# From the MLP's up products to its down products: a PSUM tile of its own for the last product, other memory for the first loads, and the last relu one step later

## The chip, the core and the metric

The kernel runs on one core of one Trainium2 chip. The metric is device time in microseconds (us), the median of the runs. Besides, one execution was recorded by the hardware profiler; its times are those of the views below. PE is TensorE's matrix multiply, PEld its weight load, DVE is VectorE, ACT is ScalarE, SP the queue that issues loads. Line numbers (L170) are those of the kernel before.

## What is computed

The reference is a two-layer trunk on a sequence of 1024 rows of width 1024, in float32. Layer 0 mixes with a gated short convolution, layer 1 with latent attention; each has an MLP with a squared relu and a hidden width of 4096.

```python
def short_conv_mixer(h, w_in, w_conv, b_conv, w_out):
    bcx = h @ w_in
    b_gate, c_gate, xh = jnp.split(bcx, 3, axis=-1)
    u = c_gate * xh
    conv = depthwise(u, w_conv) + b_conv
    return (b_gate * conv) @ w_out

def squared_relu_mlp(h, w_up, w_down):
    return jnp.square(jax.nn.relu(h @ w_up)) @ w_down

for l in range(DEPTH):
    mod = c_act @ ada_w[l] + ada_b[l]
    ...
    x = x + g_m[:, None, :] * rmsnorm(y, norm_g[l, 1])
    h = modulate(rmsnorm(x, norm_g[l, 2]), sh_f, sc_f)
    y = squared_relu_mlp(h, mlp_up_w[l], mlp_down_w[l])
    x = x + g_f[:, None, :] * rmsnorm(y, norm_g[l, 3])
```

The change lies where `h @ w_up` ends and `@ w_down` begins, once in each layer, and where `h @ w_in` of the conv mixer ends.

## The kernel before

**Precision.** Every float32 operand is split into a high part (an ACT copy, L173) and a low part (a DVE subtraction, L174). `mm` (L170) makes three matmuls of one product: low x high, high x low, high x high. The two operations of a split can only be used in that order, and a matmul waits for the part it reads.

**The up products.** `mlp_up` works on pairs of 128-column blocks of `w_up`, 16 pairs a layer. For each pair, `all_pairs` forms a 2 x 2 block product with seven products instead of eight (Winograd's scheme). A product (`prod`) is 4 x 3 = 12 matmuls with 512 columns. The operands of the activations are named "11", "21", "22", "t1" to "t4"; those of the weights are `w`, `t2`, `s2` and `t3`. After the two products of `w`, the order on PE within a pair is: product 6 (s2 with operand t2) into bank `x_`; product 7 (t3 with operand t3) into a second bank, `v`; product 5 (t2 with t1), added into `x_`; and, put off into the next pair, product 3 (`second`, t3 with 22), added into `x_`, and product 4 (`fourth`, t2 with t4), added into `v`. Between them partial sums are taken out: `take(u2)` and `take(u4)` (L581) copy `x_` on ACT after products 6 and 5, `u4 += v` follows on DVE (L594), `third` evicts `x_` after product 3 (L1217, a relu), and `last` adds `v` to `u2` (L609). Product 3 cannot start before `take(u4)` has read `x_`. PSUM has four such banks ("one"), two for each pair, used in turn.

For the last pair there is no next pair: `mlp_up` calls `second` and `fourth` at once and leaves the rest (`last`, `third`) to the down stage. `last` ends with `done`, which is `store`: two relus and two squares on ACT (L1221 to L1225), and a `late` entry whose DVE sums (L1236 to L1239) and seven stores to the DRAM arrays `ha[0]` to `ha[6]` (L1241, issued from ACT's queue) are made when `flush` is called. The conv mixer's input products run through the same `all_pairs`; there the steps of the last job are called in reverse order of the list.

**The down products.** `down_pairs` makes seven products too, in the order 0, 1, 3, 6, 4, 5, 2, each over seven steps i. A step loads a block of `w_down` into its own place (only in products 0, 1, 3, 6) and 512 KB of `ha` into one of four raw tiles, splits both into *rings* (the weight side alternates between two rings, the other side goes round three), and makes 24 matmuls into four banks. The order of SP's loads is fixed to that of the program (`pinned`). Over the first three steps a list `before` is worked off from its end, with ACT's and DVE's order fixed as written (`pinned`): each step's two splits first, then one entry. Entry of step 0: `third`, then `last` with `store`; of step 1: nothing; of step 2: `flush`. So ACT works through step 0's high parts, `third`, the relus and squares, step 1's high parts, and so on.

**The memory of the blocks.** `room` gives each block of 4 KB (per partition) its place in a pool: `sl` on the left, `sd` on the right. `sd` is laid over memory that the up stage used: from its front over the up stage's weight pool `up` (split weights, then two raw tiles that only every third pair uses, then s2), and behind that over the operands of the activations in the order "11", "21", t2, t3. A load into such a place waits for the last reader of the old contents.

**Background tasks.** `bg` is a list of tasks for the next stage's modulation vectors. For each vector eight of ten tasks load 512 KB of `ada_w` (or `kv_ada_w`) into a raw tile and add it, scaled, on DVE (L195); the last makes 16 small matmuls (L214). `down_pairs` of layer 0 has four vectors, 40 tasks; `run_bg(1 + (i % 3 == 0))` takes one or two a step in every product but the first. In layer 1 the list is empty there.

Of the kernel before, what the change touches and what calls it, by code (L numbers as in the profile page):

```python
# [17 lines left out]
P = 128  # L18
# [43 lines left out]
def trunk_kernel(ctx: ExitStack, tc: tile.TileContext, x, c, ada_w, ada_b, norm_g, conv_in_w, conv_w,  # L62
# [5 lines left out]
    def nm(s):  # L68
        uid[0] += 1
        return f"{s}_{uid[0]}"  # L70
# [176 lines left out]
    def run_bg(n):  # L247
        for _ in range(min(n, len(bg))):
            bg.pop(0)()
# [289 lines left out]
    def prod(out_, which, ops, first=True, kks=range(4)):  # L539
        w, k0, name = which  # L540
        for kk in kks:
            mm(out_, (w[0][:, k0 + kk, :], w[1][:, k0 + kk, :]), ops[name][kk], first and kk == 0, kk == 3, not first)
# [4 lines left out]
    def all_pairs(up, ops, jobs):  # L547

        end = []
        for raws, begun, quarter, done, between in jobs:
            ready = raws()
            a = begun if begun is not None else row_tile()
            p1 = a[:, HALF:] if begun is not None else None
            x_ = bank_ps()
            if begun is None:
                w = up_split(up, ready[0])  # L560
                prod(x_, (w, 0, "11"), ops)
                nc.scalar.activation(a[:, :HALF], x_, AF.Copy)
                if end:
                    end.pop()()
                y_ = mm_ps()
                prod(y_, (w, 4, "21"), ops)
                if end:
                    end.pop()()
                nc.vector.tensor_tensor(a[:, :HALF], a[:, :HALF], y_, op=ALU.add)
            rest = {}  # L570
            if isinstance(ready, dict):
                rest = ready
            else:
                for part in pair_sums(up, *ready):
                    rest.update(part or {})
            b = row_tile()
            u2, u4 = halves(b)

            def take(dst):
                if p1 is None:  # L580
                    nc.scalar.activation(dst, x_, AF.Copy)  # L581
                else:
                    nc.vector.tensor_tensor(dst, p1, x_, op=ALU.add)

            prod(x_, rest[6], ops, begun is not None)
            take(u2)
            while end:
                end.pop()()
            between()
            v = bank_ps()  # L590
            prod(v, rest[7], ops)
            prod(x_, rest[5], ops, False)
            take(u4)
            nc.vector.tensor_tensor(u4, u4, v, op=ALU.add)  # L594

            def second(x_=x_, rest=rest):
                prod(x_, rest[3], ops, False)

            def third(x_=x_, p1=p1, a=a, quarter=quarter):
                if p1 is None:  # L600
                    quarter(a, x_)
                else:
                    nc.vector.tensor_tensor(p1, p1, x_, op=ALU.add)

            def fourth(v=v, rest=rest):
                prod(v, rest[4], ops, False)

            def last(v=v, u2=u2, a=a, b=b, done=done):
                nc.vector.tensor_tensor(u2, u2, v, op=ALU.add)  # L609
                done(a, b)  # L610

            end += [last, third, fourth, second]
        return end

    def up_mm(w, h, kk=KD, steps=None):
# [169 lines left out]
    def down_pairs(ys, wd, before):  # L785

        sd = pool("sd", "right")  # L790
        n = PAIRS // 2
        w4 = wd[ROWS * P:, :].rearrange("(q two p) d -> p q two d", two=2, p=P)
        sl = pool("sl")
        ws = [{} for _ in range(n)]

        def room(q, b, i0, i1):
            for i in range(i0, i1):
                ws[i][b] = q.tile([P, 2, HALF], F32, name=nm("w"))

        room(sl, "12", 0, n)  # L800
        room(sl, "11", n - 5, n)
        room(sd, "22", 0, n)
        room(sd, "21", 1, n)
        rings = [sd.tile([P, 2, 2, HALF], F32R, name=nm("ring")) for _ in range(5)]
        room(sd, "11", 0, n - 5)
        room(sd, "21", 0, 1)
        pbs = [rings[2], rings[0]]
        spares = [rings[1], rings[3], rings[4]]
        pas = [spares[(7 * n - 1 - j) % 3] for j in range(3)]
        count = 0  # L810

        def get(i, b):
            ld(ws[i][b], w4[:, 2 * i:2 * i + 2, int(b[0]) - 1, (int(b[1]) - 1) * HALF:int(b[1]) * HALF])

        def less(i, b, x_, y_):
            nc.vector.tensor_tensor(ws[i][b], ws[i][x_], ws[i][y_], op=ALU.subtract)

        def spot(half, t, col):
            return ys[4 * half + t][:, col * HALF:(col + 1) * HALF]

        def copy(half, col):
            return lambda t, p_: nc.scalar.activation(spot(half, t, col), p_, AF.Copy)

        def add(half, col):
            return lambda t, p_: nc.vector.tensor_tensor(spot(half, t, col), spot(half, t, col), p_, op=ALU.add)

        def sums(t, p_):
            u = spot(1, t, 0)
            nc.vector.tensor_tensor(u, u, p_, op=ALU.add)
            for half in range(2):  # L830
                nc.vector.tensor_tensor(spot(half, t, 1), spot(half, t, 1), u, op=ALU.add)

        with pinned([mybir.EngineType.SP]):
            for which, one, more, b, make, done in (
                    (0, True, False, "11", None, copy(1, 0)),
                    (1, True, True, "21", None, copy(0, 0)),
                    (3, False, False, "12", "11", copy(1, 1)),
                    (6, False, True, "22", None, copy(0, 1)),
                    (4, True, False, "22", "12", sums),
                    (5, False, False, "11", "t3", add(1, 1)),  # L840
                    (2, False, True, "21", "22", add(1, 0))):
                if not more:
                    banks_ = [bank_ps() for _ in range(4)] if one else [mm_ps(), mm_ps(), tp_ps(), tp_ps()]
                    spare[0] = mm_ps if one else bank_ps
                if which == 2:
                    sl.release()
                    arb = pool("arB")
                    first = slots_of(arb, 3)
                for i in range(n):
                    if which in (0, 1, 3, 6):  # L850
                        get(i, b)
                    if make == "t3":
                        less(i, "11", "22", "11")
                    elif make:
                        less(i, b, b, make)
                    raw = raw_tile().rearrange("p (q m) -> p q m", q=2)
                    ld(raw, ha[which][2 * i:2 * i + 2].rearrange("q p m -> p q m"))
                    pa, pb = pas[count % 3], pbs[count % 2]
                    count += 1
                    with pinned([mybir.EngineType.Activation, mybir.EngineType.DVE]) if before else nullcontext():  # L860
                        split_w(pa[:, 0], pa[:, 1], raw)
                        split_w(pb[:, 0], pb[:, 1], ws[i][b])
                        if before:
                            before.pop()()
                    if which == 2 and i >= n - 3:
                        fill_row(first[i - n + 3], wd, from_dram(hd), i - n + 3)
                    if which:
                        run_bg(1 + (i % 3 == 0))
                    for t in range(4):
                        ts_ = slice(t * P, (t + 1) * P)  # L870
                        for q in range(2):
                            mm(banks_[t], (pa[:, 0, q, ts_], pa[:, 1, q, ts_]), (pb[:, 0, q], pb[:, 1, q]),
                               i == 0 and q == 0 and not more, i == n - 1 and q == 1, more)
                        if i == n - 1:
                            done(t, banks_[t])
        run_bg(99)
        spare[0] = mm_ps
        sd.release()
        ara = pool("arA", "right")
        return [ara, arb, pool("arC")], first + slots_of(ara, 3)[::-1]  # L880
# [329 lines left out]
    def mlp_up(l, up, ops, firsts, per_pair_bg):  # L1210
# [36 lines left out]
        def between(i):  # L1247
            flush()
            if i >= AHEAD:
# [2 lines left out]
        store(0, ca[0], cb)  # L1252
        end = all_pairs(up, ops, [(lambda i=i: ready if i == 1 else load_pair(mlp_up_w[l], i, up), ca[i] if i < AHEAD else None, quarter,
                                   lambda a, b, i=i: store(i, a, b), lambda i=i: between(i)) for i in range(1, n)])
        second, fourth = end.pop(), end.pop()
        second()
        fourth()
        run_bg(99)
        up.release()
        release_arena()  # L1260
        return [flush, lambda: None, lambda: [step() for step in end[::-1]]]

    def cols_of(w, n):
        return [w[:, m * P:(m + 1) * P] for m in range(n)]
# [405 lines left out]
```

## Time and profile before

| | us |
|---|---|
| median of three runs | 2152.4 (2151.09 to 2154.95) |
| the profiled execution | 2151.04 |
| its span, first to last instruction | 2149.3 |
| first passage, up to down, layer 0 | around 690 to 709 in the span |
| second passage, layer 1 | around 1816 to 1836 |
| end of the conv mixer's input products | around 283 to 295 |

How to read the views. A row of a timeline has the start in us from the span's start, the time, the engine, the line, the operation, what it writes and reads, the count of merged instructions, and in brackets how long the engine was idle before it and what ended that. `one`, `mm`, `tp` and `big` are PSUM tiles, `ring`, `raw`, `w`, `slot`, `q` and `y` tiles in SBUF. Matmuls overlap: a row of 12 spans 2.88 us, and the next 12 start 2.72 us after its start. SPq and ACTq rows are the issuing of DMAs by those queues; the transfer lands later.

### The profile page before, as it was taken

The page shows a single profiled execution, that of the slowest core. Times are in us where ns is not written, and L with a number is a line of the kernel's source. Part 1 is how long each engine was busy: PE and PEld are TensorE (multiplying, and loading weights), DVE is VectorE, ACT ScalarE, POOL GpSimd, SP SyncE. Part 2 cuts the span into 40 slices and gives each one's busy share as a digit, 9 for nine tenths or more (in the row PEclk, how much of TensorE's full clock was granted, in tenths as well). Part 3 has the DMA queues.
Part 4 walks back from the last instruction along what each step waited for, and adds up shares of the span by engine and source line. Part 5 has one row for each costly group of instructions (what it writes and reads, how often), then busy time and mean ns, then how long its engine had stood idle before and what let it go on. Part 6 is the DMA issues. An engine that isn't in the chain of part 4 may idle for free.

```text
span 2149.3 us, 25252 instructions
## 1 busy us (share of the span) xinstructions
PE 2083.8 (97%) x9638; PEld 1712.5 (80%) x9638; DVE 1530.3 (71%) x2063; ACT 1060.0 (49%) x1512; POOL 4.0 (0%) x8
## 2 busy tenths in 40 slices
PE   6999999999999999999899999999999999999998
PEld 5888888888888778888677888877888887788887
DVE  5877776977665677956788877765976665558556
ACT  4633354845454534344665555564845543444342
POOL 0000000000000000000000000000000000000000
PEclk9999999999999999999999999999999999999999
DMA  8344464466443976444214231043455543853243
GB/s 244 99 145 143 136 205 135 131 200 210 152 144 127 324 268 240 167 147 167 86 55 129 78 107 42 25 162 126 132 187 186 172 162 130 293 191 125 98 147 137
DMA packets 242335, 330.85 MB, mean 154 GB/s; under 512 B 18629, under 2 KB 143906, under 8 KB 242214
## 3 DMA queue, kind: packets, MB, share of 16 engines
q1 hardware_dynamic: 204328, 248.57, 36.6%
q10 hardware_dynamic: 37886, 80.67, 9.9%
q8 instruction: 76, 1.25, 0.2%
q14 instruction: 45, 0.37, 0.1%
HBM read 248.45 MB, written 80.74 MB: 153 GB/s over the span
## 4 chain that ended last, share of the span: by engine, by line
PE 73%; DVE 12%; ACT 7%; DMA 5%; issue 2%; SPq 0%; ACTq 0%; DVEq 0%
PE one L170 38%; PE mm L170 19%; PE tp L170 6%; PE big L170 4%; ACT junk L255 2%; DMA raw<-in_ada_w_dram 2%; PE big L1465 2%; DVE y L315 1%; DVE raw L316 1%; DVE acc L195 1%; PE tp L1491 1%; DMA raw<-in_kv_ada_w_dram 1%; DVE ring L174 1%; ACT small L257 1%; DVE y L309 1%
## 5 line engine op out<-in xcount | busy, mean ns | idle before, releaser
L170 PE MATMUL one<-slot,uphi 128*128 128x512 f32 x1240 | 382.0, 389 | 0.0
L170 PEld LDWEIGHTS one<-slot,uphi 128*128 128x128 f32 x1240 | 232.8, 188 | 48.5 <-issue 0.5
L170 PE MATMUL big<-slot 128*128 128x512 f32 x1152 | 265.6, 390 | 1.1 <-DVE slot L174 0.6
L170 PEld LDWEIGHTS big<-slot 128*128 128x128 f32 x1152 | 215.3, 188 | 47.0 <-DVE y L919 1.1
L170 PE MATMUL one<-slot,uplo 128*128 128x512 f32 x620 | 243.5, 393 | 3.6 <-ACT y L581 2.1
L170 PE MATMUL one<-ring,ring 128*128 128x512 f32 x1008 | 232.3, 391 | 6.2 <-DVE ring L174 6.1
L173 ACT ACTIVATE ring<-w 128x1024 fp32r<-128x1024 f32 x98 | 103.7, 1058 | 263.5 <-PE tp L170 134.0
L170 PEld LDWEIGHTS one<-ring,ring 128*128 128x128 f32 x1008 | 188.2, 188 | 49.2 <-ACT ring L173 5.6
L174 DVE TENSOR_TENSOR ring<-w,ring 128x1024 fp32r<-128x1024 f32 x98 | 119.9, 1223 | 111.5 <-ACT ring L173 111.5
L174 DVE TENSOR_TENSOR uplo<-raw,uphi 128x1024 fp32r<-128x1024 f32 x117 | 142.8, 1223 | 79.0 <-ACT uphi L173 78.9
L173 ACT ACTIVATE uphi<-raw 128x1024 fp32r<-128x1024 f32 x117 | 123.7, 1059 | 135.6 <-PE one L170 76.9
L170 PE MATMUL mm<-ring,ring 128*128 128x512 f32 x672 | 162.7, 390 | 1.0 <-DVE ring L174 1.0
L170 PE MATMUL tp<-ring,ring 128*128 128x512 f32 x672 | 161.7, 389 | 0.0
L170 PE MATMUL mm<-slot,uphi 128*128 128x512 f32 x504 | 158.3, 395 | 0.4 <-DVE slot L430 0.4
L170 PEld LDWEIGHTS mm<-ring,ring 128*128 128x128 f32 x672 | 125.6, 188 | 28.5 <-DVE ring L174 2.0
L170 PEld LDWEIGHTS tp<-ring,ring 128*128 128x128 f32 x672 | 126.1, 188 | 26.2
L195 DVE SCALAR_TENSOR_TENSOR acc<-raw,csil,acc 128x1024 f32<-128x1024 f32 x88 | 112.6, 1279 | 40.3 <-DMA raw<-in_ada_w_dram 36.0
L170 PEld LDWEIGHTS one<-slot,uplo 128*128 128x128 f32 x620 | 116.4, 188 | 30.3 <-ACT y L581 3.8
L174 DVE TENSOR_TENSOR ring<-raw,ring 128x1024 fp32r<-128x1024 f32 x98 | 119.6, 1220 | 18.1 <-ACT ring L173 18.1
L170 PE MATMUL one<-slot,s 128*128 128x512 f32 x468 | 112.6, 389 | 0.6 <-DVE s L174 0.6
L170 PEld LDWEIGHTS mm<-slot,uphi 128*128 128x128 f32 x504 | 94.8, 189 | 21.1 <-issue 1.4
L581 ACT ACTIVATE y<-one 128x512 f32<-128x512 f32 x62 | 36.7, 592 | 142.8 <-PE one L170 98.5
(271 smaller groups left out, 3486.5 us busy)
## 6 DMA issues: line engine op xcount, KB each, us to landing
ha<-y ACTq DMA_DIRECT2D x196, 256.0 KB, 3.0
raw<-ha SPq DMA_DIRECT2D x98, 512.0 KB, 4.1
raw<-in_ada_w_dram SPq DMA_DIRECT2D x80, 512.0 KB, 4.4
raw<-in_mlp_up_w_dram SPq DMA_DIRECT2D x70, 512.0 KB, 5.0
w<-in_mlp_down_w_dram SPq DMA_DIRECT2D x56, 512.0 KB, 4.9
raw<-hd SPq DMA_DIRECT2D x24, 512.0 KB, 4.5
xs<-raw ACTq DMA_DIRECT2D x24, 512.0 KB, 3.0
raw<-xs SPq DMA_DIRECT2D x24, 512.0 KB, 4.1
```

The lines of the kernel that those rows point to most:

```text
L170: nc.tensor.matmul(out_, lhs[a], rhs[b], start=first and i == 0, stop=last and i == 2, skip_group_check=more)
L173: nc.scalar.activation(hi, src, AF.Copy)
L174: nc.vector.tensor_tensor(lo, src, hi.bitcast(F32), op=ALU.subtract)
L195: nc.vector.scalar_tensor_tensor(acc, raw, s, acc, op0=ALU.mult, op1=ALU.add)
L255: nc.scalar.activation(junk, src, AF.Square, accum_out=ss)
L257: nc.scalar.activation(rt, ss, AF.Sqrt, bias=eps_d)
L309: nc.vector.tensor_tensor(y, y, p_, op=ALU.add)
L315: nc.vector.scalar_tensor_tensor(y, y, rroot(ss), self.gmb, op0=ALU.mult, op1=ALU.mult)
L316: nc.vector.tensor_tensor(xr, xr, y, op=ALU.add)
L581: nc.scalar.activation(dst, x_, AF.Copy)
L1465: nc.tensor.matmul(o_, a, m_, start=j == 0, stop=j == 4)
L1491: nc.tensor.transpose(p_[:, c:c + P], pts[4 * hf + i][:, j * P:(j + 1) * P], ident)
```

## The change

- In `all_pairs` the last job takes a further bank: `u2 += v` is done at once on DVE, `v` becomes a new bank, product 4 starts there from nothing, and it goes ahead of product 3. `last` and `done` become two steps, `last` and `finish`.
- In `mlp_up` the entry of step 1 in `before` becomes `finish` (relus, squares and the `late` entry), which step 0 did before. `flush` stays at step 2.
- In `down_pairs` the places in `sd` come in another order: "11" 0 and 1 stand right behind the "22" blocks, "21" 1 to 3 behind the rings.
- `run_bg(1)` in place of `run_bg(1 + (i % 3 == 0))`.

```diff
-        for raws, begun, quarter, done, between in jobs:
+        for n_job, (raws, begun, quarter, done, between) in enumerate(jobs):
+            final = n_job == len(jobs) - 1
...
             take(u4)
             nc.vector.tensor_tensor(u4, u4, v, op=ALU.add)
+            if final:
+                nc.vector.tensor_tensor(u2, u2, v, op=ALU.add)
+                v = bank_ps()
...
-            def fourth(v=v, rest=rest):
-                prod(v, rest[4], ops, False)
-
-            def last(v=v, u2=u2, a=a, b=b, done=done):
-                nc.vector.tensor_tensor(u2, u2, v, op=ALU.add)
+            def fourth(v=v, rest=rest, final=final):
+                prod(v, rest[4], ops, final)
+
+            def last(v=v, u2=u2):
+                nc.vector.tensor_tensor(u2, u2, v, op=ALU.add)
+
+            def finish(a=a, b=b, done=done):
                 done(a, b)

-            end += [last, third, fourth, second]
+            end += [finish, last, third, second, fourth] if final else [finish, last, third, fourth, second]
...
         room(sd, "22", 0, n)
-        room(sd, "21", 1, n)
-        rings = [sd.tile([P, 2, 2, HALF], F32R, name=nm("ring")) for _ in range(5)]
         room(sd, "11", 0, n - 5)
         room(sd, "21", 0, 1)
+        room(sd, "21", 4, n)
+        rings = [sd.tile([P, 2, 2, HALF], F32R, name=nm("ring")) for _ in range(5)]
+        room(sd, "21", 1, 4)
...
                     if which:
-                        run_bg(1 + (i % 3 == 0))
+                        run_bg(1)
...
-        second, fourth = end.pop(), end.pop()
-        second()
-        fourth()
+        for _ in range(2):
+            end.pop()()
         run_bg(99)
         up.release()
         release_arena()
-        return [flush, lambda: None, lambda: [step() for step in end[::-1]]]
+        return [flush, end.pop(0), lambda: [step() for step in end[::-1]]]
```

## The prediction

> **What bounds the kernel now.** I read the page first, for the busiest engine, then a table by stretch, then TensorE's own timeline, and at each of its gaps the timelines of the other engines.
>
> ```profile
> span 2149.3 us, 25252 instructions
> PE 2083.8 (97%) x9638; PEld 1712.5 (80%) x9638; DVE 1530.3 (71%) x2063; ACT 1060.0 (49%) x1512; POOL 4.0 (0%) x8
> 688.40:709.00 20.60, 17.49 (x74) 13.27 (x73) 7.23 (x9) 9.92 (x13) 0.00 (x0) 1.00 0.96 337
> 1815.90:1836.20 20.30, 17.35 (x74) 13.15 (x72) 7.14 (x9) 9.78 (x13) 0.00 (x0) 1.00 0.97 339
> ```
>
> PE is busy for 97% of the span, so only the stretches where it waits can be won. The last two rows are the two passages (stretch, length, busy time and count of PE, PEld, DVE, ACT, POOL, granted clock, DMA share, GB/s): PE is idle for 3 us in each while the DMA engines are full. How fast PE goes when nothing stops it, and where it stops in the first passage:
>
> ```profile
> 784.12 2.88 PE L170 MATMUL mm<-ring,ring 128*128 128x512 f32 x12
> 786.84 2.88 PE L170 MATMUL tp<-ring,ring 128*128 128x512 f32 x12
> ...
> 688.43 0.39 PE L170 MATMUL one<-slot,uplo 128*128 128x512 f32 x1
> 694.72 0.50 PE L170 MATMUL one<-slot,uplo 128*128 128x512 f32 x1 [0.69 <-ACT y L581]
> 701.41 0.70 PE L170 MATMUL one<-ring,ring 128*128 128x512 f32 x2 [0.95 <-DVE ring L174]
> 702.46 5.28 PE L170 MATMUL one<-ring,ring 128*128 128x512 f32 x22 [0.34 <-DVE ring L174]
> 708.86 49.68 PE L170 MATMUL one<-ring,ring 128*128 128x512 f32 x217 [1.12 <-DVE ring L174]
> ```
>
> Twelve matmuls take 786.84 - 784.12 = 2.72 us; a down step of 24 takes 5.44. From 688.43 (product 7 of the last pair) to 708.86 (down step i=1) PE has 72 matmuls, 16.32 us, and takes 20.43: **4.11 us lost**. They split so:
> - Products 7 and 5 should end at 688.43 + 5.44 = 693.87; product 3 starts at 694.72 (0.85), since it adds into the bank that `take(u4)` (L581) is still reading.
> - Products 3 and 4 should end at 694.72 + 5.44 = 700.16; down step 0 starts at 701.41: 1.25, waiting for the first splits.
> - Its 24 matmuls should end at 706.85; 22 of them (4.99) start at 702.46 and end at 707.45: 0.60.
> - Step 1 starts at 708.86: 1.41.
>
> ```profile
> 1815.88 0.39 PE L170 MATMUL one<-slot,uplo 128*128 128x512 f32 x1
> 1822.17 0.50 PE L170 MATMUL one<-slot,uplo 128*128 128x512 f32 x1 [0.69 <-ACT y L581]
> 1836.15 71.17 PE L170 MATMUL one<-ring,ring 128*128 128x512 f32 x312 [1.12 <-DVE ring L174]
> 282.68 0.39 PE L170 MATMUL one<-b,uplo 128*128 128x512 f32 x1
> 288.97 0.50 PE L170 MATMUL one<-slot,uplo 128*128 128x512 f32 x1 [0.69 <-ACT y L581]
> 294.55 35.77 PE L170 MATMUL big<-slot 128*128 128x512 f32 x157
> ```
>
> The second passage has the same form: 1836.15 - 1815.88 - 16.32 = **3.95 us**. The conv mixer's end runs through the same `all_pairs`: 48 matmuls (10.88) from 282.68 to 294.55, **0.99 us** lost at its one wait. In layer 0's down products there are three more waits, which layer 1's, without background tasks, do not have:
>
> ```profile
> 759.30 5.73 PE L170 MATMUL one<-ring,ring 128*128 128x512 f32 x24 [0.77 <-DVE ring L174]
> 765.64 11.36 PE L170 MATMUL one<-ring,ring 128*128 128x512 f32 x47 [0.61 <-DVE ring L174]
> 776.84 1.84 PE L214 MATMUL mm<-ones,acc 128*128 128x1 f32 x16
> 778.54 5.75 PE L170 MATMUL one<-ring,ring 128*128 128x512 f32 x24
> 851.25 0.39 PE L170 MATMUL mm<-ring,ring 128*128 128x512 f32 x1
> 852.59 2.79 PE L170 MATMUL mm<-ring,ring 128*128 128x512 f32 x11 [0.95 <-DVE ring L174]
> ```
>
> From 708.86 to 776.84 are 217 + 24 + 47 = 288 matmuls, 65.28 us, in 67.98: 2.70 lost. At 851.25 another 852.59 - 851.25 - 0.23 = 1.11. Together **3.81 us**.
>
> **The change part by part.**
>
> *Last product first, own bank.* Product 4 goes ahead of product 3, into a fourth bank. Banks rotate, so that is the one of the pair before, read long ago: no wait. Its 12 matmuls (2.72 us) cover `take(u4)`, which needs the 0.85 us. Added is one DVE add per use (u2 + v early), three in all:
>
> ```profile
> 694.07 0.60 ACT L581 ACTIVATE y<-one 128x512 f32<-128x512 f32 x1 [4.80 <-DMA ha<-y]
> 694.70 0.69 DVE L594 TENSOR_TENSOR y<-y,one 128x512 f32<-128x512 f32 x1 [3.74 <-ACT y L581]
> 702.32 0.68 DVE L609 TENSOR_TENSOR y<-y,one 128x512 f32<-128x512 f32 x1
> 700.86 0.58 ACT L1217 ACTIVATE y<-one 128x512 f32<-128x512 f32 x1
> 294.75 0.69 DVE L609 TENSOR_TENSOR y<-y,one 128x512 f32<-128x512 f32 x1 [1.44 <-PE one L170]
> ```
>
> 0.68 us each on a DVE that idled for 3.74 us there: nothing on the path. PE then runs through to 693.87 + 5.44 = 699.31, where down step 0 could start. Product 3's bank is now evicted last (L1217, before at 700.86); the second group of step 0 needs that bank at 699.31 + 1.36 = 700.67, and the eviction can run from about 699.5 to 700.1. So 0.5 us of cover; without it the price is that lateness, under 1 us. In the conv the next stage's first big tile lies on banks of that pool, so it can come to wait for the new bank's add. Unhidden, that add would end like the present one, about 295.5, 0.95 us *after* the old start; DVE idled 1.44 us ahead of it (last row), so I take the full gain. Term: -0.85 x 2 - 0.99, with +0.95 as the conv's other end.
>
> *First loads in other memory.* The queue shows what they waited for:
>
> ```profile
> 603.82 22.24 SPq L127 DMA_DIRECT2D raw<-in_mlp_up_w_dram  x4
> 691.34 0.37 SPq L127 DMA_DIRECT2D w<-in_mlp_down_w_dram  x1
> 691.80 0.81 SPq L127 DMA_DIRECT2D raw<-ha  x1
> ...
> 698.95 1.06 ACT L173 ACTIVATE ring<-raw 128x1024 fp32r<-128x1024 f32 x1 [4.28 <-DMA raw<-ha]
> 701.18 1.22 DVE L174 TENSOR_TENSOR ring<-w,ring 128x1024 fp32r<-128x1024 f32 x1
> ```
>
> SP issues nothing from 626 to 691.34, then the first block at the end of product 7 (688.43 + 2.72 + drain): blocks "11" 0 and 1 lie over operand t3, which that product reads last. The first `raw<-ha` stands behind it in the queue and lands 7.1 us later in a stretch whose DMA share is 0.96. In the new order 13 blocks of 4 KB still stand ahead of the rings (7+6 before, 7+2+1+3 after), so the rings do not move; "11" 0 and 1 become the eighth and ninth block. By the order of allocation that is where `up` keeps its own two raw tiles, last read by pair 13, two pairs earlier. The two raw tiles behind them are free after pair 14. So four loads can go out in SP's idle stretch, while the last pair is still multiplied. Behind them on SP stands "11" 2, which waits for product 5 as before. The first split is then limited by ACT's fixed order, behind `take(u4)`: raw high 694.7, weights high 695.6; on DVE behind the two adds raw low 696.0 to 697.2, weights low to 698.4. PE wants them at 699.31: 0.9 us to spare. Term: the 1.25 + 0.60 go, in passage two 3.95 - 0.85 - 1.41 = 1.69. The other end is no gain.
>
> *Relu one step later.* Now the four ACT operations stand between the splits of steps 0 and 1:
>
> ```profile
> 703.03 1.06 ACT L1221 ACTIVATE y<-y 128x1024 f32<-128x1024 f32 x1 [1.60 <-DVE y L609]
> 705.47 1.04 ACT L1225 ACTIVATE y<-y 128x1024 f32<-128x1024 f32 x1
> 706.41 1.04 ACT L173 ACTIVATE ring<-raw 128x1024 fp32r<-128x1024 f32 x1
> 708.63 1.22 DVE L174 TENSOR_TENSOR ring<-w,ring 128x1024 fp32r<-128x1024 f32 x1
> ```
>
> They hold ACT for 706.41 - 703.03 = 3.4 us, behind a 1.60 us wait for DVE. Afterwards step 1's splits follow the eviction directly: high parts 700.1 to 702.0, low parts until 703.4, and PE wants them at 704.75. The 1.41 us go, twice. What is late next: the relus run 702.0 to 705.4, so step 2's splits end at about 708.9 (wanted 710.2); then four DVE sums and seven stores, issued from ACT's queue, stand ahead of step 3's weight split, which I find done 0.2 to 0.5 us before 715.6. This is the thinnest cover; if it is gone, up to 1.41 comes back per passage.
>
> *Background.* 40 tasks (32 loads) in layer 0 ran 10 in each of four products of seven steps, two at every third step; now one per step over all six. PE's total is unchanged; the question is DVE.
>
> ```profile
> 756.83 1.28 DVE L195 SCALAR_TENSOR_TENSOR acc<-raw,csil,acc 128x1024 f32<-128x1024 f32 x1 [3.46 <-DMA raw<-in_ada_w_dram]
> 758.03 1.22 DVE L174 TENSOR_TENSOR ring<-w,ring 128x1024 fp32r<-128x1024 f32 x1
> 905.00:943.00 38.00, 38.00 (x168) 31.08 (x167) 21.94 (x25) 14.07 (x14) 0.00 (x0) 1.00 0.24 83
> ```
>
> A task's operation stood on DVE ahead of a ring split and waited 3.46 us for its own load; PE then waited for the split at 759.30. Fewer loads per step through the same four raw tiles should land in time. New work of 1.28 us per step comes into products 5 and 2 (first in the last row), where DVE is busy 21.94 of 38 us. One narrow spot lies there: product 4's last step has 12 adds, and PE takes over without slack. One task in the way costs its 1.28. Bounds: a gain of 3.81 and no gain with 1.28 lost. The waits hang on the loads that thin out, so I take 3.81 - 1.28 = 2.53.
>
> For that last term one page bears on it, in sentences the sum does without. The DMA engines moved 337 GB/s in the passage's row above. The Trainium skill ("DMA: Bandwidth & Descriptors", Where 436 GB/s comes from) puts HBM's limit for one core at about 358 GB/s. A step with two tasks asks for 4 x 0.524 MB in 5.44 us, 385 GB/s, and with one 289, so by that rule its stalls are memory's and all 3.81 go, for 2139.2; by the rows, which show a fixed order on DVE, 2.53 do.
>
> **Sum.** 4.11 + 3.95 + 0.99 + 2.53 = 11.58 us. The profiled execution took 2151.04 us, its span 2149.3 and 1.74 around it; it becomes 2139.46. It stood 1.36 below the median of the runs, 2152.4, so I expect a median of **2140.8 us**.
>
> **The rivals.**
> - *Background gives nothing* (its waits only move to other steps, as DVE's order is set in advance): 2152.4 - 9.05 = 2143.4. For it: DVE waited for such loads at steps with one task too. Against: those steps cost PE nothing.
> - *The first splits still set the start*, being behind the additional DVE add and ACT's order: 1.85 + 1.69 = 3.54 come back, 2144.3. Against it the 0.9 us to spare.
> - *The loads are not early*, because SP's order or a place still in use holds them: then step 0 starts at 701.41 whatever the products do, 0.85 x 2 + 3.54 are lost, 2146.0. The idle SP since 626 speaks against.
> - *Slower: each late task stops PE.* Twelve tasks now fall into products 5 and 2. If at each DVE stands before its split until the load lands, as at 852.59, that is 12 x 1.11 = 13.3 us, against 9.05 won and the 3.81 kept: 2156.7. It loses to the passages' gain below 0.75 us per task, and is slower beyond 0.2% from 1.11. Against it: DMA share there is 0.24 (column before the last).
> - *No change*: the DMA engines, full in the passage (share 0.96), bring the blocks of down steps 2 to 6 no sooner, and PE waits there for what it won; with the background giving nothing, the conv's 0.99 is left, 2151.4. Against it: four loads of 512 KB leave that stretch.
>
> **How the numbers follow.** Forecast 0.51, background nothing 0.16, first splits 0.10, loads not early 0.07, slower 0.07, no change 0.09. This measurement can tell about 0.2%, 4.3 us, from no change. The first four cases lie below 2148.1: with their tails 0.82 faster; 0.10 within; 0.08 slower. The low end: all 3.81 won, 2139.5, less about 1.5 as the runs shown spread, 2138. The high end takes in the third rival and part of the thin cover at step 3 (2146.0 + 2 x 1.41): 2148.8. Beyond it lie no change and slower, 0.16 together.
>
> **What would show it.** Right: PE's timeline from product 7 to the big tiles without a gap above 0.2 us in both passages and at the conv's end; SP's first two pairs of loads before 690; ACT's first `ring<-raw` right behind L581 and no wait on a DMA; L1221 after the second pair of splits; no PE wait on DVE's ring splits between 709 and 980. Wrong: a wait on DVE ring around step 0 (splits still bound) or step 3 (the stores), a wait of the first big tile at 294 on a DVE add, or new waits in products 5 and 2 after 905. If PE has no gap and the time has not fallen, my account of PE as the bound is wrong.

## The result, and the profile after

The kernel before ran in 2152.08 us (median of 5, in the same session), the kernel after in 2142.97 us (median of 5, 2141.04 to 2144.59): ratio 0.9956, with a 95% interval of 0.9941 to 0.997. In a later session the kernel after took 2141.02 us against 2152.19, ratio 0.995 (0.9936 to 0.9964). So between 9.1 and 11.2 us are won, where 11.58 were forecast.

The profiled execution of after is the slowest of its five runs, 2144.59 us. Its page begins:

```profile
span 2142.8 us, 25254 instructions
PE 2083.0 (97%) x9638; PEld 1715.1 (80%) x9638; DVE 1532.3 (72%) x2066; ACT 1060.5 (49%) x1512; POOL 4.0 (0%) x8
```

TensorE's busy time is within 0.8 us of what it was (2083.8 before), the three DVE instructions more (2066 for 2063) are the early adds. What went is idle time. TensorE's own timeline of after (start, length, line, operation, tiles, count, and in brackets the wait before it) shows where:

```profile
284.18 0.40 PE L170 MATMUL one<-b,uplo 128*128 128x512 f32 x1
295.08 5.15 PE L170 MATMUL big<-slot 128*128 128x512 f32 x22
...
689.06 0.39 PE L170 MATMUL one<-slot,uplo 128*128 128x512 f32 x1
699.94 65.67 PE L170 MATMUL one<-ring,ring 128*128 128x512 f32 x289
765.91 10.99 PE L170 MATMUL one<-ring,ring 128*128 128x512 f32 x47 [0.31 <-DVE ring L174]
778.84 2.79 PE L170 MATMUL mm<-ring,ring 128*128 128x512 f32 x11 [1.71 <-DVE ring L174]
825.16 2.79 PE L170 MATMUL mm<-ring,ring 128*128 128x512 f32 x11 [0.66 <-DVE ring L174]
977.49 5.83 PE L170 MATMUL big<-slot 128*128 128x512 f32 x25
...
1824.53 76.32 PE L170 MATMUL one<-ring,ring 128*128 128x512 f32 x336
```

From product 7 of the last pair (689.06) to down step 0 (699.94) pass 10.88 us, which is exactly its 48 matmuls; step 0 runs into step 1 and on without a gap. The conv's end is 10.90 us long (284.18 to 295.08). By stretches:

```profile
689.06:705.38 16.32, 16.32 (x74) 13.52 (x73) 8.59 (x10) 8.57 (x12) 0.00 (x0) 1.00 0.95 340
1813.65:1829.97 16.32, 16.32 (x73) 13.52 (x72) 8.59 (x10) 8.57 (x12) 0.00 (x0) 1.00 0.96 341
705.38:977.49 272.11, 269.43 (x1218) 223.17 (x1216) 200.93 (x191) 114.37 (x121) 0.00 (x0) 1.00 0.66 220
```

Both passages are TensorE's own 72 matmuls long and not a tenth more, with the DMA engines as full as before (share 0.95 and 0.96). But layer 0's down stage, from step 1 to the first big tile, still holds 2.7 us of idle time. Put side by side, in us, each stretch read from TensorE's timeline:

| stretch | before | after | after, later session |
|---|---|---|---|
| lost at the conv's end | 0.99 | 0.02 | 0.03 |
| first passage, product 7 to step 1 (16.32 without loss) | 20.43 | 16.32 | 16.32 |
| layer 0's down stage, step 1 to big | 272.74 | 272.11 | 271.61 |
| second passage | 20.27 | 16.32 | 16.32 |
| layer 1's down stage, step 1 to big | 261.82 | 261.54 | 261.53 |
| all the rest of the span | 1573.05 | 1576.49 | 1572.89 |
| span | 2149.3 | 2142.8 | 2138.7 |

The stretches won are the same in both executions of after, but for 0.5 us in layer 0's down stage; the rest differs by 3.6 us between two executions of one kernel. That goes in part with the granted clock, of which more in the last section: between the first 52 us and the last 10 it was halved in one place in the execution of before, in three and in two in those of after. One place more is worth about 1.7 us, half of 3.5 us at half speed. Most of what remains lies in waits of the attention, and its cause is not shown. So the two profiled spans are 6.5 us apart where the medians are 9.1.

### The profile page after: what moved, and what is told of

Its sections match the earlier page's. It is cut to its first block, busy times and chain, and to the rows that moved or that the text cites. A ratio compares the mean times of both kernels' runs of the same rounds, so it can differ in the third digit from the quotient of the medians.

```text
span 2142.8 us, 25254 instructions
## 1 busy us (share of the span) xinstructions
PE 2083.0 (97%) x9638; PEld 1715.1 (80%) x9638; DVE 1532.3 (72%) x2066; ACT 1060.5 (49%) x1512; POOL 4.0 (0%) x8
## 4 chain that ended last, share of the span: by engine, by line
PE 75%; DVE 12%; ACT 6%; DMA 5%; issue 2%; ACTq 0%; SPq 0%; DVEq 0%
PE one L170 40%; PE mm L170 19%; PE tp L170 7%; PE big L170 3%; ACT junk L255 2%; DMA raw<-in_ada_w_dram 2%; PE big L1471 2%; DVE y L315 1%; DVE raw L316 1%; DVE acc L195 1%; PE tp L1497 1%; DVE small L1474 1%; DVE y L309 1%; DVE pt L1501 1%; ACT small L257 1%
```

## The experiments

Eleven kernels ran, and the kernel after a second time, in three sessions on different chips. The kernel before ran in each of them, with medians of 2152.24, 2152.33 and 2152.19 us. "Stage" is layer 0's down stage from step 1 to the first big tile: 272.74 us before, 272.11 and 271.61 after.

### Each part by itself

**e1**, the kernel after with the old rhythm:

```diff
-                        run_bg(1)
+                        run_bg(1 + (i % 3 == 0))
```

> The kernel after with the background tasks in their old rhythm (two at every third step). Theory (the new rhythm is worth little, since its waits only move to other steps): median within 1 us of the kernel after, 2143 to 2144 where before has 2152.1; TensorE waits on DVE's ring splits again near product 1 of layer 0's down stage, some 3 us together. Rival (the new rhythm brings the 2.5 us of the sum, and something else took 2 us away): 2145.5 or more.

Measured 2141.89 us, ratio 0.9949 (0.9937 to 0.9962). One wait of 0.74 us on a ring split stands in product 1, no other in the stage, and the stage is *shorter*, 269.83 us. So the rhythm brings nothing here. In that the theory held; the 3 us of waits that it expected did not come. In this one execution the old rhythm is 1.8 to 2.3 us better in its stage; the medians (2141.89 against 2142.97 and 2141.02) do not tell the two apart.

**e2**, the kernel before with only the new rhythm.

> The kernel before with only the new rhythm (one background task in each step of products 1 to 6). Theory: 0.6 us faster at most, 2151.5 where before has 2152.1, the passage's waits unchanged, new waits in products 1, 3 or 6. Rival: 2.5 us faster, 2149.6.

2150.98 us, ratio 0.9994 (0.9985 to 1.0003): not told from no change. The passages lose 4.09 and 3.91 as before; the stage is 272.37, 0.37 shorter, with waits of 1.33 us at 771 and 1.04 at 783 in place of those at 759, 765 and 852.

**e3**, only the other order of products with the bank of its own: the kernel after with `room`'s order and the rhythm of before, and

```diff
-        return [flush, end.pop(0), lambda: [step() for step in end[::-1]]]
+        return [flush, lambda: None, lambda: [step() for step in end[::-1]]]
```

> The kernel before with only the other order of the last pair's products and the bank of their own (relu at step 0, first loads where they were, old rhythm). Theory (each lateness in the passage hides another): product 3's wait of 0.85 goes but down step 0 still starts when the first splits are done, so both passages keep their length; only the conv's end wins its 0.99: 2151.1 where before has 2152.1. Rival (terms add up one by one): 0.85 twice and 0.99, 2149.4.

2152.08 us, ratio 0.9998 (0.9989 to 1.0007). TensorE's timeline of e3 at down steps 0 and 1, where product 7 began at 686.89:

```profile
699.95 0.70 PE L170 MATMUL one<-ring,ring 128*128 128x512 f32 x2 [2.02 <-DVE ring L174]
700.99 5.28 PE L170 MATMUL one<-ring,ring 128*128 128x512 f32 x22 [0.34 <-DVE ring L174]
707.40 38.74 PE L170 MATMUL one<-ring,ring 128*128 128x512 f32 x169 [1.12 <-DVE ring L174]
```

Product 3's wait is gone, and the wait for the first splits is 2.02 us where it was 0.95: 707.40 - 686.89 - 16.32 = 4.19 lost, against 4.11. In the second passage of this execution the granted clock was halved from 1829.3 to 1832.8, behind the wait for the first splits, and no wait shows at step 1; yet from product 7 to the start of product 3 it is 91.08 us there against 91.28 before. At the conv's end nothing is lost any more. By the trace the theory held: alone, this part wins only there. The median does not show that 0.99 us, which is within its interval.

**e4**, only the order of memory:

```diff
         room(sd, "22", 0, n)
-        room(sd, "21", 1, n)
-        rings = [sd.tile([P, 2, 2, HALF], F32R, name=nm("ring")) for _ in range(5)]
         room(sd, "11", 0, n - 5)
         room(sd, "21", 0, 1)
+        room(sd, "21", 4, n)
+        rings = [sd.tile([P, 2, 2, HALF], F32R, name=nm("ring")) for _ in range(5)]
+        room(sd, "21", 1, 4)
```

> The kernel before with only the first down loads in the other memory. Theory: down step 0 starts when product 4 ends (about 700.2 instead of 701.4), but the four relus still stand ahead of step 1's splits and end when they did, so step 1 starts at 708.9 as before: no gain, 2152.1. Rival (terms add up): 1.85 and 1.69 are won, 2148.6.

2147.93 us, ratio 0.9981 (0.9972 to 0.9989): the theory fell. The passages lose 2.29 each, so 1.82 and 1.66 are won, as the rival said. In e4's timelines of TensorE, DVE and ScalarE, with product 7 at 690.48:

```profile
702.34 5.60 PE L170 MATMUL one<-ring,ring 128*128 128x512 f32 x24
709.09 3.16 PE L170 MATMUL one<-ring,ring 128*128 128x512 f32 x12 [1.15 <-DVE ring L174]
...
702.54 0.69 DVE L609 TENSOR_TENSOR y<-y,one 128x512 f32<-128x512 f32 x1 [2.48 <-PE one L170]
...
703.26 1.06 ACT L1222 ACTIVATE y<-y 128x1024 f32<-128x1024 f32 x1 [2.84 <-DVE y L609]
```

I had held the relus' place for fixed. They wait for DVE's last add (L609), and in the kernel before that add stood behind the late first splits, which ran until 702.4 there. With the splits early, DVE waits for TensorE instead (2.48 us), and add, relus and step 1's splits all move up. The stage is shorter too, 269.91 us, with the old rhythm.

**e5**, the kernel before with the relu one step later:

```diff
-            def last(v=v, u2=u2, a=a, b=b, done=done):
+            def last(v=v, u2=u2):
                 nc.vector.tensor_tensor(u2, u2, v, op=ALU.add)
+
+            def finish(a=a, b=b, done=done):
                 done(a, b)
...
-        return [flush, lambda: None, lambda: [step() for step in end[::-1]]]
+        return [flush, end.pop(0), lambda: [step() for step in end[::-1]]]
```

> The kernel before with only the last pair's relu and stores one step later. Theory: down step 0 starts at 701.4 with its 0.6 us gap as before, but step 1's splits now stand right behind the evictions, so its wait of 1.41 goes in both passages: 2152.2 - 2.8 = 2149.4. Rival (the loads of step 1, which went out behind the late first ones, then set its start): no gain, 2152.

2149.32 us, ratio 0.9986 (0.9977 to 0.9995), as expected by the theory:

```profile
701.75 0.70 PE L170 MATMUL one<-ring,ring 128*128 128x512 f32 x2 [0.91 <-DVE ring L174]
702.80 43.58 PE L170 MATMUL one<-ring,ring 128*128 128x512 f32 x191 [0.34 <-DVE ring L174]
```

Step 0 starts late as before and runs into step 1 without a gap: 2.64 and 2.55 us are lost in the passages instead of 4.11 and 3.95.

**e6**, the kernel after with relu and stores back at step 0 (the `return` of e3).

> The kernel after with relu and stores back at step 0. Theory: the four relus (3.4 us of ScalarE) can start only when product 3 is evicted, near 700.7, so step 1's splits end near 707.4 where TensorE wants them at 705.4: 2.0 us per passage come back, 4.0 in all, 2147 where after has 2143. Rival (with the loads early, the relu's step no longer matters): 2143. If the terms of the sum simply add, 1.41 per passage: 2145.8.

2143.18 us, ratio 0.9957 (0.9945 to 0.997): by the time alone the rival. The trace says otherwise. TensorE and ScalarE in e6:

```profile
706.28 71.23 PE L170 MATMUL one<-ring,ring 128*128 128x512 f32 x312 [0.91 <-DVE ring L174]
...
700.46 1.05 ACT L1228 ACTIVATE y<-y 128x1024 f32<-128x1024 f32 x1
703.83 1.05 ACT L173 ACTIVATE ring<-raw 128x1024 fp32r<-128x1024 f32 x1
```

The relus hold ScalarE from 700.46 to 703.83, step 1 starts 1.07 us late in both passages (2.0 were expected, 1.41 by the plain sum), and about as much is given back in layer 0's stage, which takes 269.70, 1.9 to 2.4 us less than in after. In this one execution, then, what is won in the passage and what the stage loses are not independent: with a start one microsecond later, the wait at 778 is 0.46 us instead of 1.71.

### The stage with the background tasks

In after, DVE's timeline ahead of the longest wait reads:

```profile
772.16 1.23 DVE L823 TENSOR_TENSOR w<-w,w 128x1024 f32<-128x1024 f32 x1
776.43 1.23 DVE L823 TENSOR_TENSOR w<-w,w 128x1024 f32<-128x1024 f32 x1 [3.04 <-DMA w<-in_mlp_down_w_dram]
777.57 1.22 DVE L174 TENSOR_TENSOR ring<-w,ring 128x1024 fp32r<-128x1024 f32 x1
```

DVE makes two subtractions of weight blocks one after the other, stands 3.04 us at the second for its block, and only then makes the split that TensorE waits for. Four kernels try what follows from that.

**e9**, the blocks of products 1, 3 and 6 loaded a step earlier:

```diff
+        ahead = [(i, b) for b in ("21", "12", "22") for i in range(n)]
...
-                    if which in (0, 1, 3, 6):
+                    if which == 0:
                         get(i, b)
+                    elif ahead:
+                        for _ in range(2 if count == n else 1):
+                            get(*ahead.pop(0))
```

> The kernel after with the weight blocks of products 1, 3 and 6 loaded one step earlier (each block has memory of its own). Theory: the wait of 1.87 us at 777, which the profile puts down to DVE's subtraction waiting for a weight block, goes, and nothing takes its place: 2141.1. Rival (the queue is only reordered, and the task's and the activations' loads come later by as much): 2143 to 2145, with waits of L195 in place of L823's.

2142.5 us, ratio 0.9952 (0.9939 to 0.9964); stage 270.87. The wait of TensorE there is 1.77 us, no smaller. DVE in e9:

```profile
749.26 1.23 DVE L824 TENSOR_TENSOR w<-w,w 128x1024 f32<-128x1024 f32 x1
...
774.97 1.23 DVE L824 TENSOR_TENSOR w<-w,w 128x1024 f32<-128x1024 f32 x1 [3.19 <-DMA w<-in_mlp_down_w_dram]
```

The first subtraction now stands at 749.26 where it was 756.56 in after: DVE's order is settled when the program is built, and it put the subtractions ahead by as much as the loads. The earlier load bought nothing. The theory fell, the rival's reason (other loads late instead) was not seen either.

**e11**, each subtraction kept behind the splits of the step before by a dependency that only fixes the order on DVE:

```diff
+        behind = []
+
+        def newest():
+            return [ins for ins in nc.cur_bb.bb.instructions if ins.engine == mybir.EngineType.DVE][-1]
+
         def less(i, b, x_, y_):
             nc.vector.tensor_tensor(ws[i][b], ws[i][x_], ws[i][y_], op=ALU.subtract)
+            tc.add_manual_dep(newest(), behind[-1], NO_SYNC, reason="less")
...
                         split_w(pb[:, 0], pb[:, 1], ws[i][b])
+                        behind.append(newest().name)
```

> The kernel after with each subtraction of weight blocks kept behind the ring splits of the step before on DVE, so that none runs two steps ahead. Theory (at 776 DVE stood at a subtraction that nobody needed yet, ahead of a split that TensorE waited for): the wait of 1.71 goes, from down step 1 to the big tiles 270.3 instead of 272.1, median 2141.2. Rival (the block is late whatever the order): 272, 2143.

2146.17 us, ratio 0.9968 (0.9956 to 0.998), slower than after. No wait is left at 778, as the theory said: TensorE runs from step 0 to 903 without one on a ring. But a loss turns up elsewhere. The stage takes 271.48 us; about 1.7 of that is a halved clock from 903 to 906.6, behind a wait of 0.34 us for a split, and without it, if it covers no wait, the stage would be near the 270.3 of the theory (an estimate). In layer 1 the loss is plain. TensorE and DVE in e11 behind the change from product 4 to product 5 of layer 1:

```profile
2022.15 0.70 PE L170 MATMUL mm<-ring,ring 128*128 128x512 f32 x2 [1.15 <-ACT ring L173]
2024.33 2.56 PE L170 MATMUL mm<-ring,ring 128*128 128x512 f32 x10 [1.02 <-DVE ring L174]
...
2018.45 0.69 DVE L844 TENSOR_TENSOR y<-y,y 128x512 f32<-128x512 f32 x1
2019.05 0.68 DVE L844 TENSOR_TENSOR y<-y 128x512 f32<-128x512 f32 x1
2019.65 1.22 DVE L828 TENSOR_TENSOR w<-w,w 128x1024 f32<-128x1024 f32 x1
```

Product 4 ends with twelve sums on DVE (L842 and L844). The subtraction that was made two steps ahead had been out of their way; now it stands behind them, ends at 2020.9 and both splits are late. Layer 1's down stage takes 263.84 us instead of 261.54. The early subtraction harmed one place and served another. The median is 3.2 to 5.2 us above those of after, and these 2.3 us are the part of it that the trace explains.

**e8**, no task in product 1, eight in each of the five products after it:

```diff
-                    if which:
-                        run_bg(1)
+                    if which > 1 or count > 2 * n:
+                        run_bg(1 + (i == 3))
```

> The kernel after with the background tasks starting at the third product of the down stage (product 3) instead of the second, eight in each of five products. Theory (the waits come from DVE standing at late loads in its fixed order, and the loads are late while the passage's traffic and the weight blocks fill the queue, in products 1 and 3): the waits at 765 and 778 of the kernel after go, 2 us less from down step 1 to the big tiles (270 instead of 272.1), 2141. Rival (the waits only move to products 3 and 6): 2143 or more.

2139.87 us, ratio 0.9943 (0.9929 to 0.9956), the fastest kernel of the study. The stage of e8, and product 1 in after and in e8 (length, TensorE, weight loads, DVE, ScalarE, GpSimd, clock, DMA share, GB/s):

```profile
704.84:974.33 269.49, 269.49 (x1217) 223.00 (x1216) 200.97 (x191) 113.96 (x121) 0.00 (x0) 1.00 0.66 222
```

```profile
738.10:776.80 38.70, 38.39 (x170) 31.38 (x168) 25.63 (x23) 16.23 (x18) 0.00 (x0) 1.00 0.81 267
```

```profile
737.50:775.60 38.10, 38.10 (x170) 31.55 (x169) 24.37 (x21) 16.24 (x18) 0.00 (x0) 1.00 0.58 194
```

TensorE is busy for the whole 269.49 us. In product 1 the DMA share falls from 0.81 to 0.58, and DVE's waits for weight blocks, summed over the stage (total, times, longest; after, then e8), all but vanish:

```profile
DVE w L823 <- DMA w<-in_mlp_down_w_dram: 6.0, 2, 3.0
```

```profile
DVE w L823 <- DMA w<-in_mlp_down_w_dram: 0.4, 1, 0.4
```

The theory held: nothing moved to products 3 and 6 at a price. The interval of the time overlaps with those of after, so that the 1.2 to 3.1 us between the medians are not settled by them; the 2.1 to 2.6 us in the stage are read from one execution of e8, and e13 has as short a stage from the kernel before.

**e12**, e8 and e11 together.

> Both together: subtractions behind the splits of the step before, background tasks from product 3 on. Theory: nothing is left to wait for but late tasks' loads in product 3; from step 1 to the big tiles 268.7 to 269.5 (layer 1's 261.5 and four times 1.8 us of TensorE's own work for the tasks), median 2139 to 2140. Rival (the subtractions then come too late for their splits): above 270, 2141 or more.

2146.57 us, ratio 0.9969 (0.9957 to 0.998); stage 273.13, layer 1's 265.42: the rival. DVE has the sums, the subtractions and the tasks behind one another, and TensorE waits for splits in four places between 901 and 967.

**e13**, the kernel before with only e8's rhythm.

> The kernel before with only the background tasks moved: none in product 1, eight in each of the five after it. Theory (what costs is tasks in product 1, whose loads queue behind the passage's): 2.5 to 3.3 us won, 2149.3 where before has 2152.2, the passage's own 4.1 and 4.0 unchanged. Rival (only the earlier first loads free the queue for it): no more than 1 us, 2151.2.

2148.62 us, ratio 0.9987 (0.9977 to 0.9997), 3.6 us by the medians; the stage 269.70, 3.0 shorter, and the passages 4.05 and 3.91 as ever: the theory. One row of TensorE's timeline in e13 covers product 0 from step 1 and all of product 1, where before it was cut at 759 and 765:

```profile
710.83 71.17 PE L170 MATMUL one<-ring,ring 128*128 128x512 f32 x312 [1.12 <-DVE ring L174]
```

**after_again**, the kernel after unchanged.

> The kernel after, unchanged, a second time. Theory: median 2142 to 2143.5; its down stage from step 1 to the big tiles takes 272 us again, with waits near 778 and 824 that differ by tenths, and the places where the granted clock halves differ from those of the first execution. Rival (the down stage's loss differs from execution to execution): 270 or less.

2141.02 us, below what was expected; stage 271.61, with the wait at 778.86 again (1.85 us), that at 765.84 larger (0.60 us) and none at 825. So the large wait came in both executions, the small ones vary. The granted clock was halved near 280 and 1027 in both, near 1413 in the first alone.

## Why the prediction came out as it did

**The passages (4.11 + 3.95 forecast).** Right, to the last hundredth: 16.32 us are left of 20.43 and of 20.27. The three parts were costed as independent terms, and the single runs bear this out for two: the loads 1.82 and 1.66 (e4; 1.85 and 1.69 forecast), the relu 1.47 and 1.40 (e5; 1.41 each). The third, the own bank, was to bring 0.85 and alone brings nothing: the wait for the first splits takes its place (e3). Added to the early loads it brings 1.22 in each passage (2.29 lost in e4, 1.07 in e6), and the relu, added to both, the last 1.07. So what a part is worth hangs on the order in which the parts are added: 1.82 + 1.22 + 1.07 is the 4.11 of the first passage as much as 0.85 + 1.85 + 1.41 is. The total was safe, since it was all that could be lost there and every part of it went. Early loads with the late relu and without the bank were not run.

**The loads.** Right in the outcome, wrong in a step. Four loads were to leave in SP's idle stretch; two did:

```profile
675.97 0.37 SPq L127 DMA_DIRECT2D w<-in_mlp_down_w_dram  x1
685.85 0.37 SPq L127 DMA_DIRECT2D raw<-ha  x1
691.56 0.37 SPq L127 DMA_DIRECT2D w<-in_mlp_down_w_dram  x1
692.23 0.39 SPq L127 DMA_DIRECT2D raw<-ha  x1
```

The second block went out at 691.56, when the first one had gone in the kernel before (691.34). What holds it is not settled: it goes 2.50 to 2.52 us behind the start of product 7 in after, after_again, e1 and e4, as if that product still used its place, while the view of SP's waits names the stores `ha<-y` of the pair before. One pair is all that step 0 needs, and step 1's pair landed in time for ScalarE at 700.63.

**The thin covers.** All held. ScalarE and DVE in after:

```profile
695.19 1.05 ACT L173 ACTIVATE ring<-raw 128x1024 fp32r<-128x1024 f32 x1
700.13 0.60 ACT L1224 ACTIVATE y<-one 128x512 f32<-128x512 f32 x1 [2.95 <-PE one L170]
700.63 1.05 ACT L173 ACTIVATE ring<-raw 128x1024 fp32r<-128x1024 f32 x1
702.53 1.04 ACT L1228 ACTIVATE y<-y 128x1024 f32<-128x1024 f32 x1
...
697.66 1.22 DVE L174 TENSOR_TENSOR ring<-w,ring 128x1024 fp32r<-128x1024 f32 x1
714.46 1.23 DVE L174 TENSOR_TENSOR ring<-w,ring 128x1024 fp32r<-128x1024 f32 x1 [1.22 <-ACT ring L173]
```

The first splits end at 697.66 + 1.22 = 698.88, 1.06 ahead of step 0 (0.9 forecast), and ScalarE's first one waits for no load. Product 3's bank is evicted at 700.73; step 0's second group wants it at 699.94 + 1.36 = 701.30, 0.57 later (0.5). The relus start behind step 1's splits. Step 3's weight split ends at 715.69 and step 3 starts at 705.38 + 2 x 5.44 = 716.26: 0.57 (0.2 to 0.5).

**The conv's end (0.99).** Right: 0.02 is left, and the first big tile waits for no add. The profiled execution of after loses 1.44 us one product earlier, to the clock (4.31 us from product 6 to product 7, where before has 2.87).

**The background (2.53).** Here a step failed: "Fewer loads per step through the same four raw tiles should land in time". The stage won 0.63 and 1.13 us, and alone (e2) 0.37; the rival to which I gave 0.16, that the waits only move to other steps, is what happened in this term, and its 2143.4 is nearer to the 2142.97 of the first session than the forecast. Not even the 0.63 and 1.13 are shown to be the rhythm's, for e1 has the shorter stage without it. That the other session's 2141.02 lies so close to the forecast of 2140.8 is no credit to this term. With one task per step in product 1 the DMA engines are still at a share of 0.81 there, and DVE in its fixed order meets late loads as before, among them a weight block that the prediction had not counted. To leave product 1 without tasks is enough to end the waits: in e8 and e13 they are gone, and the stage takes 269.5 and 269.7 us, so that 3.0 of the 3.81 us were to be had. But it is not the only way, and a full queue in product 1 does not by itself cost time. In e4 the tasks start in product 1 at the old rhythm, the share there is 0.75 at 248 GB/s (0.73 and 248 before), DVE stands at weight blocks for 5.4 us in three waits, just as before, and yet TensorE waits for no split in the whole stage (269.91). Why the old rhythm does well with the loads early (e1, e4) and badly without (272.74) stays open; e6, where a shift of 1.07 us made the new rhythm's stage 2 us shorter, suggests that it is a matter of when the late loads fall, which no run isolates. By the limit of 358 GB/s in the Trainium skill ("DMA: Bandwidth & Descriptors", Where 436 GB/s comes from) all 3.81 would have gone at one task per step; the trace does not agree, product 1 moved 267 GB/s and waited. Nor was 358 GB/s a bound here: over the 10 us from 1825 the kernel before moved 392 GB/s. (That case comes to 2139.5 by the prediction's own terms, not to the 2139.2 written there.)

**The sum.** With the terms as the second execution of after shows them, 0.96 + 4.11 + 3.95 + 1.13, and 0.29 in layer 1's stage, it is 10.44; its span is 10.6 shorter than that of before. By the stretches the forecast was 1.1 too much, by the medians 2.5 and 0.4 (9.11 and 11.17 won). The background term is too large by 1.4 to 1.9, even if all that the stage won is put down to it; layer 1's 0.29 was not forecast.

The rivals that spoke of late loads, of first splits and of a full queue in steps 2 to 6 fell with the gapless passages, and so did the slower one: in the stage of after no wait on a ring split stands behind the one at 825, and products 5 and 2 come later. Two of the signs named for being right did not appear: SP's second pair of loads left behind 690, and TensorE did wait on ring splits between 709 and 980.

## What to carry to other kernels

A chain of small waits at one passage is worked out from what each step would meet if the one ahead of it were early, and each part is worth trying alone: here one part of three was worth nothing by itself and 1.22 us behind another. In the stage with the background tasks, on an engine with an order settled in advance, thinning out the tasks (e2) or loading the weight blocks a step earlier (e9) did not help, and forcing the order moved the loss to another place; to keep the optional work out of the product behind the passage did (e8: 269.49 us, TensorE never idle). Where two medians of the same program are 2 us apart, here 2142.97 and 2141.02, changes of that size are better read stretch by stretch from the traces.

## What the runs showed of the hardware

The granted clock fell to half for about 3.5 us at a time (for 7 us once each in e3, e6 and e13), in places that differ between executions. Before and after, at product 6 of the conv's last pair:

```profile
279.81:282.60 2.79, 2.79 (x12) 2.32 (x13) 2.26 (x3) 1.04 (x2) 0.00 (x0) 1.00 0.82 295
```

```profile
279.87:282.60 2.73, 2.73 (x7) 2.17 (x8) 2.26 (x3) 0.98 (x2) 0.00 (x0) 0.50 0.77 272
279.50:283.00 3.50, 3.13 (x7) 2.51 (x8) 3.03 (x4) 1.67 (x3) 0.00 (x0) 0.51 0.72 263
283.00:283.50 0.50, 0.50 (x4) 0.39 (x3) 0.50 (x3) 0.50 (x1) 0.00 (x0) 0.98 1.13 328
```

In after TensorE ran seven matmuls in the time of twelve; half of 3.5 us, 1.7, is what such a stretch takes from a TensorE that is full. What stands ahead of it is the same in both:

```profile
277.36 1.84 PE L214 MATMUL mm<-ones,acc 128*128 128x1 f32 x16
279.87 4.48 PE L170 MATMUL one<-slot,s 128*128 128x512 f32 x12 [0.67 <-DVE s L174]
```

sixteen matmuls of one column and a wait of 0.67 us, 2.5 us with little work. The same place was halved in eleven of the fourteen profiled executions and not in the other three, whether or not the conv's code was changed; most of the others lie near 1030, 1068, 1135 and 1413, in the attention, where TensorE waits often. Between the first 52 us and the last 10 there are one to five such places in an execution. The three that stand alone, at 1829 in e3, 903 in e11 and 2022 in e12, also begin within or right behind a wait of TensorE (1.48 and 0.34 us; 0.34 us behind sixteen matmuls of one column; 1.15 and 1.02 us). Other such waits, as at 701 and 1828 in the kernel before, were not followed by a fall. The Trainium skill ("TensorE: Matmul & The Clock Gate", Part 1: The HAM clock gate) has the clock decided in windows of about 3.4 us that run freely, with half speed after an idle one. The length agrees with the trace, and so does its coming in some executions and not in others; the pause here was shorter than such a window. In e13's profile five such places, one of them twice as long, lie within a span of 2151.7 us, while its median is 2148.62: differences of two microseconds between single profiles of this kernel mean little without the granted clock beside them.
